# A trunk of two layers on one core: the norm factors spread by two products of rounded parts

## The chip, the core and the metric

The kernel runs on one core of a Trainium2 chip. A core has a matrix engine (TensorE, PE in the profile), three engines for elementwise work (VectorE as DVE, ScalarE as ACT, GpSimd as POOL) and queues that move data between the chip's memory and the core's on-chip memory. Each engine works through its own list of instructions in order and waits where an operand isn't ready. The metric is the time of one execution in microseconds (us), the median of several runs; lower is better.

## The reference, cut to what matters

The program is a decoder of two layers over 512 tokens of 1024 features. Each layer has a mixer (a convolution module in the first, differential attention in the second), a SwiGLU feed-forward, and a gate on a per-layer embedding. Feed-forward and gate begin with an RMS norm, and it is these norms that the change is about.

```
def rms_norm(x, g):
    xf = x.astype(jnp.float32)
    y = xf * lax.rsqrt(jnp.mean(xf * xf, axis=-1, keepdims=True) + EPS)
    return (y * g.astype(jnp.float32)).astype(x.dtype)
...
        u = rms_norm(h, ffn_norm_g[i])
        h = h + swiglu(u, ffn_w_gate[i], ffn_w_up[i], ffn_w_down[i])
        gate = jax.nn.sigmoid(rms_norm(h, ple_norm_g[i]) @ ple_w_gate[i])
        h = h + gate * (p[i] @ ple_w_proj[i])
```

The factor `rsqrt(mean(x*x) + EPS)` is one number for each token.

## The kernel before, in words

**Layout.** The hidden state lies transposed, as eight tiles `h[0]` to `h[7]` of 128 features by 512 tokens. A large product is made chunk by chunk of the output: `acc` in the matrix engine's result memory (a bank of tag `mm`, of which there are four) collects eight chunks of the input. Every fp32 operand is split into a rounded part `hi` and a rest `lo`, both of type `fp32r`, and `mm3` makes one chunk from three `fp32r` products: lines 166 (`lo` weights with `hi` input), 167 (`hi` with `hi`) and 168 (`hi` with `lo`). A weight tile is loaded to `wraw` (two buffers), rounded by ScalarE to `whi` (line 159, four buffers) and subtracted by VectorE to `wlo` (line 161, four buffers).

**The norm.** The products are made from the input times the gain, without the factor, and the factor is multiplied onto the result. `Norm.chunk` squares each chunk and GpSimd adds the squares up in `acc`. `columns` (line 199) multiplies four blocks of 128 tokens of `acc` with a matrix of ones, so that each token's sum stands in a partition; `rsqrt_cols` makes a 128x4 tile `r` of factors of it (VectorE, line 265; GpSimd's power, line 267). To have the factors along the free axis in all partitions, `diagonal` (line 272) multiplies the identity by the four columns of `r`, which gives a 128x512 tile of four diagonal blocks (a `wk` buffer), and `spread` (line 282) multiplies it with ones: each of the 128 rows of the result `tp` then holds all 512 factors. `rows` copies it to `rb` (ScalarE, line 257).

**Who uses it.** Five norms take this way: the first norm of all (the convolution's, through `diagonal` directly), and two in each layer by `Norm.diagonal` and `Norm.rows`: the feed-forward's, within the first pair of gate and up products of `ffn`, and the gate's, in `ple` behind its first two products. In `ffn`, `rb` is needed by lines 869 and 871, which take the results `pg` (gate) and `pu` (up) of a chunk out of their banks; in `ple` by line 912. While `rb` isn't there, the matrix engine goes on with the next chunks until the four banks are full. Lines 667 to 685 (`Operands.chunk`) prepare later operands from `rb` in the same stretch.

**Order.** A scheduler that estimates times when the program is built sets the order on each engine; on the chip each engine keeps that order. Tiles of one tag share a fixed number of buffers, and an instruction that writes a buffer waits for the readers of what it held before.

Of the kernel before, what the change touches and what calls it, by code (L numbers as in the profile page):

```python
# [12 lines left out]
F32 = mybir.dt.float32  # L13
F32R = mybir.dt.float32r
AF = mybir.ActivationFunctionType
ALU = mybir.AluOpType
# [4 lines left out]
P = 128  # L21
# [70 lines left out]
def trunk(ctx, tc, xT, pT, wts, diag, dww, vec, rel, onehot, lamv, out):  # L92
    nc = tc.nc
    V, A, G, T = nc.vector, nc.scalar, nc.gpsimd, nc.tensor
# [7 lines left out]
    def sb(shape, tag, bufs, dt=F32):  # L102
        uid[0] += 1
        return pool.tile(shape, dt, tag=tag, name=f"{tag}_{uid[0]}", bufs=bufs)
# [8 lines left out]
    wk = lambda dt=F32, shape=(P, S): sb(list(shape), "wk", 4, dt)  # L113
    big = lambda dt=F32, shape=(P, S): sb(list(shape), "big", 5, dt)
    f = lambda ap: ap.bitcast(F32)
# [12 lines left out]
    ones_r = sb([P, P], "ones", 1, F32R)  # L128
    ones = f(ones_r)
# [4 lines left out]
    t = wk()[:, 0:P]  # L134
# [4 lines left out]
    t = tp()  # L139
# [69 lines left out]
    class Norm:  # L209
# [39 lines left out]
            return rsqrt_cols(first_of(t), 4, 1.0 / D)  # L249

        def diagonal(self):
            self.dg = diagonal(self.columns())

        def rows(self):

            r = sb([P, S], "rb", 1)
            A.copy(r, spread(self.dg))
            return r
# [4 lines left out]
    def rsqrt_cols(src, n, inv):  # L263
        v = sb([P, P // 2], "v8", 2)[:, :8]
        last_v[0] = V.tensor_scalar(v[:, :n], src, inv, EPS, ALU.mult, ALU.add)
        r = sb([P, P // 2], "r8", 2)[:, :8]
        last_pow[0] = G.tensor_tensor(r[:, :n], v[:, :n], mhalf[:, :n], ALU.pow)
        return r[:, :n]

    def diagonal(r):  # L270
        dg = wk()
        V.tensor_tensor(
            dg.rearrange("p (b t) -> p b t", b=4),
            ident.unsqueeze(1).to_broadcast([P, 4, P]),
            r.unsqueeze(2).to_broadcast([P, 4, P]),
            ALU.mult,
        )
        return dg

    def spread(dg):  # L280
        t = tp()
        T.matmul(t, ones, dg, start=True, stop=True)  # L282
        return t


# [205 lines left out]
    for c in range(NC):  # L491
        wa, wg = pairs[c]
        if c == 0:
            pg = half(wg)
            pa = half(wa)
            norm.dg = diagonal(norm.columns_of_chunks(3))
            rb = norm.rows()
# [81 lines left out]
    r = rsqrt_cols(vs[:, 0:4], 4, 1.0)  # L579
# [4 lines left out]
    dg = wk()  # L584
# [360 lines left out]
    rl = sb([33, NH], "big", 5)  # L945
# [6 lines left out]
    for k in range(2):  # L952
        t = tp()
# [447 lines left out]
```

## Time and profile before

| what | value |
|---|---|
| median of 3 runs | 1247.7 us (1247.47 to 1248.56) |
| the profiled execution | 1246.62 us, of it 1244.5 us from the first instruction to the last (the span) |
| PE busy | 1234.6 us (99% of the span) |
| DVE busy | 877.2 us (70%) |
| ACT busy | 623.7 us (50%) |
| POOL busy | 469.7 us (38%) |
| spreads by line 282 | 5, recorded as 10 matmuls |
| diagonals by line 272 | 5, 0.69 us each |

A busy engine is one that works on an instruction; shares over the whole span hide that stages differ. A row of the timeline has the start, the duration, the engine, the line, the operation, what it writes and reads, and in brackets how long the engine had been idle and what ended the wait. A line number is that of the kernel before; the changed kernel's lines from 250 on stand five to nine lines lower (its spread by two products is line 291, its diagonal 277, its copy to `rb` 262, and 878 and 880 are what 869 and 871 were).

### The profile page before, as it was taken

To read this page: it belongs to the slowest core of one execution; us is meant where nothing else is said; L and a number is where in the kernel's file an instruction comes from. 1 tells how busy PE (TensorE), PEld (TensorE's weight loads), DVE (VectorE), ACT (ScalarE), POOL (GpSimd) and SP (SyncE) were. 2 spreads that over 40 slices of the span, in tenths; PEclk is the share of its full clock that TensorE was granted. 3 is DMA by queue.
4 is the path that set the end of the run, shared out by engine and by line. 5 is a ranking of instruction groups with operands and counts; after the bars stand their busy time and mean duration, and the time that the engine had idled before them with its cause. 6 is when DMAs were issued, how large, how long until landed. Compare 5 with 4: busy or idle time off the path is not lost.

```text
span 1244.5 us, 18421 instructions
## 1 busy us (share of the span) xinstructions
PE 1234.6 (99%) x7080; PEld 1081.8 (87%) x7080; DVE 877.2 (70%) x1230; ACT 623.7 (50%) x1096; POOL 469.7 (38%) x355
## 2 busy tenths in 40 slices
PE   9999999999999999999999999999999999999998
PEld 8888788888998899888888888788889998999887
DVE  6997865975895478547676876647966885588535
ACT  6652454533553255434566877735434552455432
POOL 3863432024670464132336635141026640562220
PEclk9999999999999999999999999999999999999999
DMA  7566224224323332334432330152232333232331
GB/s 267 185 213 195 77 57 121 90 100 125 96 92 119 102 94 77 102 104 152 124 114 80 104 100 29 52 153 85 90 127 90 102 114 109 83 102 87 104 98 67
DMA packets 49154, 136.33 MB, mean 110 GB/s; under 512 B 5635, under 2 KB 10243, under 8 KB 49068
## 3 DMA queue, kind: packets, MB, share of 16 engines
q1 hardware_dynamic: 46944, 131.74, 34.0%
q10 hardware_dynamic: 2124, 3.43, 0.9%
q8 instruction: 55, 0.90, 0.3%
q14 instruction: 31, 0.25, 0.1%
HBM read 128.84 MB, written 6.31 MB: 109 GB/s over the span
## 4 chain that ended last, share of the span: by engine, by line
PE 96%; DVE 2%; issue 1%; ACT 0%; POOL 0%; DVEq 0%; ACTq 0%; POOLq 0%
PE mm L166 29%; PE mm L167 29%; PE mm L168 29%; PE sc L398 2%; PE mm L1117 1%; PE tp L199 1%; PE sc L1085 1%; PE sc L1084 1%; PE tp L1104 1%; PE mm L398 1%; PE tp L1038 1%; PE mm L354 1%; DVE wlo L711 0%; PE tp L282 0%; PE tp L141 0%
## 5 line engine op out<-in xcount | busy, mean ns | idle before, releaser
L159 ACT CAST whi<-wraw 128x1024 fp32r<-128x1024 f32 (+2 forms) x145 | 145.6, 1013 | 218.3 <-PE mm L168 96.7
L161 DVE TENSOR_TENSOR wlo<-wraw,whi 128x1024 fp32r<-128x1024 f32 (+2 forms) x141 | 179.2, 1277 | 69.4 <-ACT whi L159 69.1
L166 PE MATMUL mm<-A,wlo 128*128 128x512 f32 (+1 forms) x568 | 222.1, 391 | 0.1
L167 PE MATMUL mm<-A,whi 128*128 128x512 f32 (+1 forms) x568 | 219.5, 387 | 0.0
L168 PE MATMUL mm<-A,whi 128*128 128x512 f32 (+1 forms) x568 | 217.3, 389 | 0.0
L166 PE MATMUL mm<-B,wlo 128*128 128x512 f32 x352 | 137.0, 389 | 0.0
L167 PE MATMUL mm<-B,whi 128*128 128x512 f32 x352 | 137.0, 389 | 0.0
L168 PE MATMUL mm<-B,whi 128*128 128x512 f32 x352 | 135.6, 389 | 0.0
L229 POOL TENSOR_TENSOR acc<-acc,wk 128x512 f32<-128x512 f32 x35 | 58.4, 1670 | 193.4 <-ACT wk L228 192.9
L166 PEld LDWEIGHTS mm<-A,wlo 128*128 128x128 f32 x568 | 106.8, 188 | 23.1 <-issue 1.4
L167 PE MATMUL mm<-C,whi 128*128 128x256 f32 x448 | 126.8, 283 | 0.0
L168 PE MATMUL mm<-C,whi 128*128 128x256 f32 x448 | 126.8, 283 | 0.0
L166 PE MATMUL mm<-C,wlo 128*128 128x256 f32 x448 | 126.8, 283 | 0.0
L167 PEld LDWEIGHTS mm<-A,whi 128*128 128x128 f32 x568 | 106.9, 188 | 22.0 <-issue 1.0
L168 PEld LDWEIGHTS mm<-A,whi 128*128 128x128 f32 x568 | 106.5, 188 | 22.0 <-issue 0.5
L711 DVE TENSOR_TENSOR wlo<-A,whi 128x1024 fp32r<-128x1024 f32 x60 | 105.7, 1769 | 19.1 <-ACT whi L710 19.1
L710 ACT CAST whi<-A 128x1024 fp32r<-128x1024 f32 x60 | 62.9, 1048 | 54.5 <-PE mm L168 43.3
L720 POOL TENSOR_TENSOR A<-wraw 128x512 f32<-128x512 f32 x16 | 22.5, 1408 | 170.4 <-DMA wraw<-in_wts 156.1
L720 POOL TENSOR_TENSOR A<-A 128x512 f32<-128x512 f32 x16 | 25.2, 1575 | 162.3 <-DMA A<-in_wts 162.3
L167 PEld LDWEIGHTS mm<-C,whi 128*128 128x128 f32 x448 | 86.0, 192 | 0.2
L166 PEld LDWEIGHTS mm<-C,wlo 128*128 128x128 f32 x448 | 86.0, 192 | 0.2
L168 PEld LDWEIGHTS mm<-C,whi 128*128 128x128 f32 x448 | 86.0, 192 | 0.0
(309 smaller groups left out, 3031.2 us busy)
## 6 DMA issues: line engine op xcount, KB each, us to landing
wraw<-in_wts SPq DMA_DIRECT2D x161, 512.0 KB, 3.6
A<-in_wts SPq DMA_DIRECT2D x32, 512.0 KB, 3.6
wraw<-in_wts SPq DMA_DIRECT2D x16, 384.0 KB, 3.1
D<-in_diag SPq DMA_DIRECT2D x22, 256.0 KB, 4.6
C<-in_diag SPq DMA_DIRECT2D x16, 256.0 KB, 5.1
h<-in_xT SPq DMA_DIRECT2D x8, 256.0 KB, 5.3
rest<-h SPq DMA_DIRECT2D x8, 256.0 KB, 2.4
bias<-scr ACTq DMA_DIRECT2D x8, 256.0 KB, 3.6
```

The lines of the kernel that those rows point to most:

```text
L159: A.copy(hi[:, cut], raw[:, cut])
L161: eng.tensor_tensor(lo[:, cut], raw[:, cut], f(hi[:, cut]), ALU.subtract)
L166: T.matmul(acc, al, bh, start=first, stop=False, **kw)
L167: T.matmul(acc, ah, bh, start=False, stop=False, **kw)
L168: return T.matmul(acc, ah, bl, start=False, stop=last, **kw)
L199: r = T.matmul(t[:, cut], src[:, cut], ones, start=first and b == 0, stop=last and b == 3)
L229: self.last = self.eng.tensor_tensor(self.acc, self.acc, sq, ALU.add)
L354: last_tap[0] = T.matmul(acc, dg[:, j % 4], ups[c][:, j : j + S], start=(j == 0), stop=(j == PE_TAPS[c] - 1))
L398: last_tap[0] = T.matmul(acc[:, g * P : (g + 1) * P], w, ups[c][:, g, LEAD - m : LEAD - m + P], start=(m == 0), stop=(m == LAGS - 1),)
L710: A.copy(hi, src)
L711: V.tensor_tensor(lo, src, f(hi), ALU.subtract)
L720: G.tensor_tensor(s[:, 0], r1[:, 0], r1[:, 1], ALU.add)
```

## The change

For the four norms of feed-forwards and gates, the 128x4 tile of factors is split into a rounded part `rh` and a rest `rl`; a diagonal is made of each, of type `fp32r`, and the spread is two `fp32r` products that add up in one bank. The first norm keeps the one fp32 product.

```
         def diagonal(self):
-            self.dg = diagonal(self.columns())
+            r = self.columns()
+            rh = sb([P, P // 2], "r8", 2, F32R)[:, :4]
+            rl = sb([P, P // 2], "v8", 2)[:, :4]
+            V.tensor_copy(rh, r)
+            V.tensor_tensor(rl, r, f(rh), ALU.subtract)
+            self.dg = diagonal(f(rh), F32R), diagonal(rl, F32R)
...
-    def diagonal(r):
-        dg = wk()
+    def diagonal(r, dt=F32):
+        dg = wk(dt)
         V.tensor_tensor(
             dg.rearrange("p (b t) -> p b t", b=4),
...
     def spread(dg):
         t = tp()
-        T.matmul(t, ones, dg, start=True, stop=True)
+        if not isinstance(dg, tuple):
+            T.matmul(t, ones, dg, start=True, stop=True)
+            return t
+        for i, d in enumerate(dg):
+            T.matmul(t, ones_r, d, start=i == 0, stop=i == 1)
         return t
```

The scheduler moves some instructions with it. On PE, at the first layer's feed-forward, `mm_1860` is the second chunk's gate product `pg`, `mm_1861` its `pu`, and `tp_1836` the spread. Before:

```order
L168 MATMUL mm_1860<-A_314_1714,whi_1849 128x512
L282 MATMUL tp_1836<-wk_1809,ones_70 128x512
L166 MATMUL mm_1860<-A_320_1752,wlo_1850 128x512
L167 MATMUL mm_1860<-A_320_1752,whi_1849 128x512
L168 MATMUL mm_1860<-A_320_1752,whi_1849 128x512
L166 MATMUL mm_1861<-A_286_1549,wlo_1856 128x512
```

Now, where the same two banks are called `mm_1867` and `mm_1868`:

```order
L168 MATMUL mm_1867<-A_314_1714,whi_1856 128x512
L166 MATMUL mm_1867<-A_320_1752,wlo_1857 128x512
L167 MATMUL mm_1867<-A_320_1752,whi_1856 128x512
L291 MATMUL tp_1842<-wk_1813,ones_70 128x512
L168 MATMUL mm_1867<-A_320_1752,whi_1856 128x512
L291 MATMUL tp_1842<-wk_1815,ones_70 128x512
L166 MATMUL mm_1868<-A_286_1549,wlo_1863 128x512
```

The spread's first product stands two products later than the one spread did, and its second behind the last product of the gate chunk.

On DVE, at the same place: `r` and `v` are the small 128x4 tiles, `wk` the diagonals, `wlo` the weights' rests, and lines 869 and 871 the first to use `rb`. Before:

```order
L265 TENSOR_SCALAR v_335_1805<-tp_1800 128x4
L161 TENSOR_TENSOR wlo_1939<-wraw_1937,whi_1938 128x1024
L272 TENSOR_TENSOR wk_1809<-ident_65,r_336_1807 128x512
L161 TENSOR_TENSOR wlo_1945<-wraw_1943,whi_1944 128x1024
L869 TENSOR_TENSOR big_1839<-mm_1774,rb_1835 128x512
L871 TENSOR_TENSOR big_1840<-mm_1775,rb_1835 128x512
L869 TENSOR_TENSOR big_1910<-mm_1860,rb_1835 128x512
L667 SCALAR_TENSOR_TENSOR B_354_1919<-h_7_87,vec_63,rb_1835 128x512
L667 SCALAR_TENSOR_TENSOR B_354_1919<-h_11_91,vec_63,rb_1835 128x512
L161 TENSOR_TENSOR wlo_2027<-wraw_2025,whi_2026 128x1024
```

Now:

```order
L270 TENSOR_SCALAR v_335_1805<-tp_1800 128x4
L161 TENSOR_TENSOR wlo_1946<-wraw_1944,whi_1945 128x1024
L255 CAST r_337_1809<-r_336_1807 128x4
L256 TENSOR_TENSOR v_338_1810<-r_336_1807,r_337_1809 128x4
L277 TENSOR_TENSOR wk_1813<-ident_65,r_337_1809 128x512
L277 TENSOR_TENSOR wk_1815<-ident_65,v_338_1810 128x512
L161 TENSOR_TENSOR wlo_1952<-wraw_1950,whi_1951 128x1024
L161 TENSOR_TENSOR wlo_2034<-wraw_2032,whi_2033 128x1024
L878 TENSOR_TENSOR big_1846<-mm_1774,rb_1841 128x512
L880 TENSOR_TENSOR big_1847<-mm_1775,rb_1841 128x512
L878 TENSOR_TENSOR big_1917<-mm_1867,rb_1841 128x512
```

Three instructions are new, and one subtraction of weights (`wlo_2027`, now `wlo_2034`) has moved from behind the first uses of `rb` to ahead of them.

On ACT, the copy to `rb` and the rounding of the same weight change places. Before:

```order
L159 CAST whi_1938<-wraw_1937 128x1024
L159 CAST whi_1944<-wraw_1943 128x1024
L257 COPY rb_1835<-tp_1836 128x512
L159 CAST whi_2026<-wraw_2025 128x1024
L870 ACTIVATE big_1839<-big_1839 128x512
```

Now:

```order
L159 CAST whi_1945<-wraw_1944 128x1024
L159 CAST whi_1951<-wraw_1950 128x1024
L159 CAST whi_2033<-wraw_2032 128x1024
L262 COPY rb_1841<-tp_1842 128x512
L879 ACTIVATE big_1846<-big_1846 128x512
```

The rounding now stands ahead of the copy. The other three norms change in the same way, the gates' with line 912 in the place of 869 and 871. In the lists of VectorE and ScalarE neighbours trade places over the 20 to 60 instructions behind each of these norms; all else keeps its order, GpSimd's list and the transfers' among it.

## The prediction

> **What bounds the kernel now.** I read the page first, its busy times, its slices and its chain.
>
> ```profile
> PE 1234.6 (99%) x7080; PEld 1081.8 (87%) x7080; DVE 877.2 (70%) x1230; ACT 623.7 (50%) x1096; POOL 469.7 (38%) x355
> ...
> PEclk9999999999999999999999999999999999999999
> ...
> PE 96%; DVE 2%; issue 1%; ACT 0%; POOL 0%; DVEq 0%; ACTq 0%; POOLq 0%
> ```
>
> The matrix engine works for 99% of the span at its full granted clock, and 96% of the chain that ended last is its own work. So a microsecond of matrix work that is taken out anywhere should come off the time, unless something else is late right behind it. The view of waits, for PE alone, tells how much else is late: seven groups, of which the first and two more are
>
> ```profile
> PE tp L141 <- POOL ident masks.py:199: 1.5, 1, 1.5
> PE sc L1084 <- DVE st L1087: 1.3, 2, 1.0
> ...
> PE mm L166 <- DVE big L768: 0.4, 1, 0.4
> ```
>
> None is at a norm's spread. The chain in order of time shows what the spreads cost on PE, beside two ordinary products:
>
> ```profile
> 27.84 0.86 PE tp L282 x2
> 171.76 0.45 PE mm L168 x2
> 217.35 0.86 PE tp L282 x2
> 565.89 0.86 PE tp L282 x2
> 862.01 0.86 PE tp L282 x2
> 1210.96 0.86 PE tp L282 x2
> ```
>
> All five spreads lie on the chain, with no wait in between. Each fp32 product of 128x512 appears as two records and takes 0.86 us of PE; two `fp32r` products of the same shape take 0.45 us.
>
> **The change part by part.** *The products.* Four of the five spreads (all but the one at 27.84) become two `fp32r` products each, with the same ones as weights. Such a product was never made with ones, but line 168's rows are of the same type, shape and number of columns, so I price it by them. A new pair costs 0.45 us and an old spread 0.86: 0.41 us saved each, 4 x 0.41 = 1.64 us. The bounds: if the second product came with the price of half an fp32 product, 0.43, the pair would cost 0.86 and nothing would be saved; if products between others gained as much as the neighbours of the old spread lose, the row of the product behind it helps:
>
> ```profile
> 216.97 0.39 PE L168 MATMUL mm<-A,whi 128*128 128x512 f32 x1
> 217.19 1.02 PE L282 MATMUL tp<-wk,ones 128*128 128x512 f32 x2
> 218.29 0.40 PE L167 MATMUL mm<-A,whi 128*128 128x512 f32 x1
> ```
>
> From the start at 216.97 to that at 218.29 are 1.32 us, in which two ordinary products (the L168 and an L166 that has a blurred record) and the spread were begun; two at 0.225 leave 0.87. So 0.42 us is the most: 1.68 us. I take 0.41.
>
> One page of the Trainium skill bears on this. "FP8 and Floating Point Precision", section "TensorE Precision Notes", has a true fp32 product make four passes through the array and the reduced one a single pass. By that rule the old spread would cost four of the trace's product steps, 4 x 0.227 = 0.91, and the saving would be 1.81 us instead of 1.64. The trace's 0.86 decides.
>
> *The chain to the diagonals.* VectorE gets three more instructions for each norm: a 128x4 rounding, a 128x4 subtraction and a second 128x512 diagonal. At the first feed-forward it looked so:
>
> ```profile
> 210.54 0.16 DVE L265 TENSOR_SCALAR v<-tp 128x4 f32<-128x4 f32 x1 [3.64 <-PE tp L199]
> 210.79 1.02 POOL L267 TENSOR_TENSOR r<-v,mhalf 128x4 f32<-128x4 f32 x1 [4.43 <-DVE v L265]
> 211.00 1.23 DVE L161 TENSOR_TENSOR wlo<-wraw,whi 128x1024 fp32r<-128x1024 f32 x1 [0.29 <-ACT whi L159]
> 212.14 0.69 DVE L272 TENSOR_TENSOR wk<-ident,r 128x512 f32<-128x512 f32 x1
> 214.21 1.22 DVE L161 TENSOR_TENSOR wlo<-wraw,whi 128x1024 fp32r<-128x1024 f32 x1 [1.39 <-ACT whi L159]
> 218.87 0.69 DVE L869 TENSOR_TENSOR big<-mm,rb 128x512 f32<-128x512 f32 x1 [3.43 <-ACT rb L257]
> 221.99 1.22 DVE L161 TENSOR_TENSOR wlo<-wraw,whi 128x1024 fp32r<-128x1024 f32 x1
> 224.06 0.42 DVE L680 TENSOR_TENSOR wtl<-B,wth 128x256 fp32r<-128x256 f32 x1
> ```
>
> The trace has no 128x4 rounding; the nearest row is L265's 0.16 us, and a 128x256 operation, 64 times as wide, took 0.42. So the two small ones cost 0.3 to 0.85 us and the second diagonal 0.69: 1.0 to 1.55 us, and I take 1.0. The second diagonal is then ready at 212.14 + 0.69 + 1.0 = 213.8 (at most 214.4). The scheduler begins the two products two and four products later than the old spread, at about 217.65 and 218.1. The margin is 3.7 us or more, so no product waits. On VectorE the 1.0 us and the weights' subtraction behind it (at 214.21 before) end by 216.5, in the 3.43 us of idle time that the row at 218.87 shows. That idle time is the cover; without it, the 1.0 us would push everything behind.
>
> *The factors come later.* This is the part that speaks against the change. On ScalarE the rounding of a weight now stands ahead of the copy to `rb`, and that rounding waited for PE:
>
> ```profile
> 218.25 0.59 ACT L257 COPY rb<-tp 128x512 f32<-128x512 f32 x1 [4.07 <-PE tp L282]
> 219.00 1.05 ACT L159 CAST whi<-wraw 128x1024 fp32r<-128x1024 f32 x1 [0.16 <-PE mm L168]
> ```
>
> It rewrites the weight buffer of the chunk in work, and so waits for that chunk's last product (L168), which now begins at 217.88 and ends about 0.39 later, so the rounding runs from 218.35 to 219.4. The copy ends at about 219.95 where it ended at 218.84: `rb` is 1.1 us late. On VectorE the subtraction that used to run at 221.99 is now ahead of L869 and ends at 220.55 (1.13 us to the next start). L869 then starts at 220.55 instead of 218.87, 1.7 us late, of which 1.13 is work only moved. Behind it wait the banks: the third chunk's gate product needs the bank that L869 empties, and began here:
>
> ```profile
> 224.22 0.39 PE L166 MATMUL mm<-A,wlo 128*128 128x512 f32 x1
> ```
>
> It would now begin at 224.22 - 0.41 = 223.8, and L869 ends at 221.2. The margin falls from 4.7 us to 2.6, and nothing waits. The weight's `lo` is made earlier than before, never later.
>
> *Where VectorE catches up.* It is 0.55 us behind, and PE 0.41 ahead, so it has to make good about 1 us. The busy times in the stretch behind the spread (columns: stretch, length, then PE, PEld, DVE, ACT, POOL busy, with counts) and a row of VectorE's timeline after it show where:
>
> ```profile
> 218.00:256.00 38.00, 38.00 (x169) 31.40 (x168) 36.06 (x59) 19.50 (x28) 0.00 (x0) 1.00 0.29 86
> 267.94 0.69 DVE L871 TENSOR_TENSOR big<-mm,rb 128x512 f32<-128x512 f32 x1 [3.57 <-PE mm L168]
> ```
>
> VectorE has 1.9 us free in the stretch, more than its lag, and by 267.94 it stands idle for 3.57 us, waiting for PE. From there on it starts when PE lets it, so the lag is gone and what follows moves ahead with PE.
>
> *The gates.* There the same exchange delays `rb` by as much, but the table load behind it was waiting anyway:
>
> ```profile
> 567.41 1.89 DVE L912 TENSOR_TENSOR big<-mm,rb 128x512 f32<-128x512 f32 x3 [3.88 <-ACT rb L257]
> 568.61 1.28 ACT L913 ACT_TABLE_LOAD   x1
> ...
> 1223.46 0.69 DVE L912 TENSOR_TENSOR big<-mm,rb 128x512 f32<-128x512 f32 x1 [1.06 <-PE mm L168]
> 1228.90 0.69 DVE L912 TENSOR_TENSOR big<-mm,rb 128x512 f32<-128x512 f32 x1 [2.63 <-PE mm L168]
> ```
>
> In the last gate VectorE waits for PE again from 1223.46 on, so the end of the program follows PE and keeps the saving.
>
> *The sum.* 4 x 0.41 = 1.64 us off, everything else hidden. The profiled execution took 1246.62 us (span 1244.5), so it would take 1244.98. The median of the three runs is 1247.7, 1.1 above that execution; against it, which is what will be measured, the forecast is 1247.7 - 1.64 = 1246.06, so 1246.1 us, 0.13% faster. About 0.2% (2.5 us) is what a measurement of this kernel can tell from no change, so this counts as the same.
>
> **The rivals.** *The saving is lost in the stretch where VectorE sets the pace.* At the end of the second part of the first feed-forward the chain leaves PE:
>
> ```profile
> 355.13 0.14 PE mm L168
> 355.35 1.06 ACT whi L710
> 373.73 0.34 DVE big L768
> 374.12 0.39 PE mm L166
> ```
>
> For 19 us the chain is VectorE's and ScalarE's, and PE waits 0.4 at its end. If VectorE's lag reached that far, what the first feed-forward saves would be lost there, and in the second layer likewise: 2 x 0.41 kept, 1246.9 us. Against it: the 3.57 us in which VectorE waits for PE in between, and that this chain begins with a PE product, so it moves ahead with PE.
>
> *The new products are no cheaper.* If `fp32r` products whose operand VectorE has just written in two halves, or which stand between others, cost 0.43 each, the time stays at 1247.7. The chain's 0.45 for two speaks against it.
>
> *Slower: the banks fill up.* If `rb` came so late that L869 emptied its bank after the third chunk wants it, PE would stand still at all four norms. The point from which this decides is a further 2.6 us of delay at a norm; to lose 2.5 us over all, the four waits have to add up to 2.5 + 1.64 = 4.1 us, so 3.6 us of further delay each. That gives 1247.7 - 1.64 + 4 x 1.1 = 1250.5. The new instructions cost 1.55 us at most and the waited-for PE product is known, so little speaks for it. GpSimd, from which VectorE could have to wait for a result, is not busy in the stretch from 218 to 256 (0.00).
>
> *More than 0.2% faster.* PE's waits behind VectorE could shrink with the new order. The 0.4 us above and as much in the second layer would bring 1247.7 - 1.64 - 0.8 = 1245.3; with the half microsecond by which medians of such runs differ (the three runs span 1.1) it crosses the bound.
>
> **How the numbers follow.** Forecast as worked out, 0.70 (1246.1, by itself 1245.2 to 1247.0); half the saving lost, 0.08 (1246.9); none saved, 0.04 (1247.7); slower by full banks, 0.06 (1250.5); faster with fewer waits, 0.12 (1244.8 to 1245.3). The range for 8 in 10 takes in the cases from 1244.7 to the 1248.3 that no saving and a slow median would give. Faster by over 0.2% (below 1245.2): the last case and a little of the forecast's spread, 0.14. Slower by over 0.2% (above 1250.2): 0.06. Within: 0.80.
>
> **What the profile after should show.** The four pairs on the chain with about 0.23 us a product, in the place of 0.86; L282's line left once, at 27.8. VectorE's diagonals ending 3 us or more ahead of the first product. `rb` about 1.1 us later behind its last product's place, L878 at the first feed-forward near 220.5, and PE with no wait there or at the third chunk. The third chunk's first product near 223.8, and everything behind earlier by 0.41, 0.82, 1.23 and 1.64 us. The prediction is wrong if PE waits for line 878 or 921 or for a diagonal, if a product of the pair takes 0.4, or if the shift shrinks between two norms.

## The result, and the profile after

The kernel after took 1246.28 us (median of 22 runs, 1244.99 to 1248.15); the kernel before, run beside it, 1248.41 us (median of 22, 1246.12 to 1252.41). The ratio is 0.998, with a 95% interval of 0.9973 to 0.9986: faster by 2.1 us between the medians and by 2.5 us by the ratio, whose interval is 1.7 to 3.4. The forecast was 1246.1 us and 1.64 us less than before.

The profiled execution of the kernel after seems to say otherwise. Its span is as long as that of before, 1244.7 us against 1244.5. These are the first rows of its page, the chain's shares, and two rows of PE's waits (PE's line, what it waited for, us in total, times, longest):

```profile
span 1244.7 us, 18430 instructions
...
PE 1232.4 (99%) x7080; PEld 1080.8 (87%) x7080; DVE 882.1 (71%) x1242; ACT 623.8 (50%) x1096; POOL 471.1 (38%) x355
...
PE 88%; DVE 4%; issue 2%; DMA 1%; ACT 0%; SPq 0%; POOL 0%; DVEq 0%; ACTq 0%
```

```profile
PE sc L407 <- DMA C<-pi: 1.7, 1, 1.7
...
PE mm L166 <- DVE big L777: 0.6, 2, 0.4
```

PE's busy time fell by 2.2 us, but it waited 1.7 us in the convolution for a transfer, which it did not do in the profile of before. The convolution ends with column sums on PE. The chain in order of time has them at these starts, in before and in after:

```profile
145.81 0.89 PE sc L199 x8
```

```profile
147.58 0.89 PE sc L199 x8
```

So after was 1.77 us late before it came to the first instruction that differs. From there to the end of the span are 1244.5 - 145.81 = 1098.7 us before and 1244.7 - 147.58 = 1097.1 after: 1.6 us less. The experiments are read by that stretch, since what lies ahead of it varies by itself.

The saving also arrives where the forecast had it, one step at each norm. The first feed-forward's column sums begin at 209.84 us before and at 211.65 after, 1.81 us late. With that taken off, the first gate's column sums begin 0.41 us earlier than before, those of the attention's norm, behind the first gate's spread, 0.86, the last gate's 1.21, and the end of the span comes 1.6 us earlier. Forecast were 0.41, 0.82, 1.23 and 1.64.

The new products are where the order put them, with the price of ordinary ones. The chain at the first feed-forward's norm, and at the first gate's:

```profile
219.39 0.23 PE mm L167
219.62 0.23 PE tp L291
219.85 0.23 PE mm L168
220.07 0.23 PE tp L291
220.30 0.23 PE mm L166
```

```profile
567.53 0.23 PE tp L291
568.21 0.23 PE tp L291
```

And what VectorE and ScalarE do at the first feed-forward, to be read against the rows of before after taking off the 1.8 us:

```profile
213.96 0.16 DVE L255 CAST r<-r 128x4 fp32r<-128x4 f32 x1
214.15 0.17 DVE L256 TENSOR_TENSOR v<-r,r 128x4 f32<-128x4 f32 x1
214.23 0.68 DVE L277 TENSOR_TENSOR wk<-ident,r 128x512 fp32r<-128x512 f32 x1
214.84 0.69 DVE L277 TENSOR_TENSOR wk<-ident,v 128x512 fp32r<-128x512 f32 x1
216.03 1.23 DVE L161 TENSOR_TENSOR wlo<-wraw,whi 128x1024 fp32r<-128x1024 f32 x1 [0.51 <-ACT whi L159]
221.24 1.23 DVE L161 TENSOR_TENSOR wlo<-wraw,whi 128x1024 fp32r<-128x1024 f32 x1 [3.99 <-ACT whi L159]
222.38 0.68 DVE L878 TENSOR_TENSOR big<-mm,rb 128x512 f32<-128x512 f32 x1
```

```profile
220.16 1.05 ACT L159 CAST whi<-wraw 128x1024 fp32r<-128x1024 f32 x1 [4.16 <-PE mm L168]
221.11 0.58 ACT L262 COPY rb<-tp 128x512 f32<-128x512 f32 x1
```

The second diagonal is ready at 215.53 and its product begins at 220.07. The copy to `rb` stands behind the weight's rounding, which waits for PE, and L878 behind that weight's subtraction. VectorE is idle for 3.99 us ahead of that subtraction all the same.

### The profile page after: what moved, and what is told of

Read it like the earlier page. It is cut to its first block, busy times and chain, and to the rows that moved or that the text cites. A ratio compares the mean times of both kernels' runs of the same rounds, so it can differ in the third digit from the quotient of the medians.

```text
span 1244.7 us, 18430 instructions
## 1 busy us (share of the span) xinstructions
PE 1232.4 (99%) x7080; PEld 1080.8 (87%) x7080; DVE 882.1 (71%) x1242; ACT 623.8 (50%) x1096; POOL 471.1 (38%) x355
## 4 chain that ended last, share of the span: by engine, by line
PE 88%; DVE 4%; issue 2%; DMA 1%; ACT 0%; SPq 0%; POOL 0%; DVEq 0%; ACTq 0%
PE mm L166 27%; PE mm L167 27%; PE mm L168 27%; PE mm L1126 1%; DVE sc L458 1%; PE sc L1094 1%; PE sc L1093 1%; PE tp L1113 1%; PE sc L407 1%; PE mm L407 1%; PE tp L1047 1%; PE mm L363 1%; PE tp L199 1%; DVE wlo L720 0%; DVE wlo L161 0%
```

## The experiments

All times are compared with runs of the kernel before on the same chip. The yardstick from the traces is the time from the convolution's column sums to the end of the span. In the kernel before it is 1098.7 us, in its repetition 1098.9; the differences are against 1098.8. Its own variation can be read from the table: where the four spreads are those of before it lies between 1098.4 and 1099.0, where they are those of after it is 1097.1 three times.

| kernel | ratio to before (95%) | column sums at | end of span | between | difference |
|---|---|---|---|---|---|
| before, again | 0.9996 (0.9987 to 1.0005) | 148.14 | 1247.0 | 1098.9 | +0.1 |
| after | 0.998 (0.9973 to 0.9986) | 147.58 | 1244.7 | 1097.1 | -1.7 |
| after, again | 0.9983 (0.9974 to 0.9991) | 148.01 | 1245.1 | 1097.1 | -1.7 |
| hi only | 0.9974 (0.9963 to 0.9984) | 147.24 | 1242.9 | 1095.7 | -3.1 |
| fp32 twice | 1.0028 (1.0016 to 1.0039) | 147.41 | 1249.4 | 1102.0 | +3.2 |
| VectorE's part only | 0.9998 (0.9989 to 1.0007) | 150.18 | 1249.2 | 1099.0 | +0.2 |
| power three times | 0.999 (0.9981 to 0.9999) | 147.60 | 1245.2 | 1097.6 | -1.2 |
| power five times | 1.0024 (1.0015 to 1.0033) | 148.68 | 1250.1 | 1101.4 | +2.6 |
| all five norms | 1.0001 (0.9992 to 1.001) | 149.75 | 1246.8 | 1097.1 | -1.7 |
| first norm only | 1.0022 (1.0013 to 1.003) | 150.46 | 1248.9 | 1098.4 | -0.4 |
| row sums, fp32 | 0.9976 (0.9965 to 0.9987) | 148.37 | 1243.0 | 1094.6 | -4.2 |
| row sums, two fp32r | 0.9951 (0.9938 to 0.9965) | 149.71 | 1243.2 | 1093.5 | -5.3 |

**The kernel before, unchanged.**

> The kernel before itself, unchanged, as a control. Products theory (the time moves by what the spreads' products cost on PE and by nothing else): ratio to before 1.000 within 0.07%. Rival, the convolution's transfers: in the profile of the kernel after, the first feed-forward's column sums began 1.81 us later than in the profile of before (211.65 against 209.84), though no instruction ahead of that place differs. If transfers within one execution do that, this kernel's profile too shows the column sums some tenths to 2 us away from 209.84, with the spreads still 0.86 us each.

The ratio is that of no change, and the profile's column sums begin 2.33 us later than in the first profile of the same code:

```profile
148.14 0.89 PE sc L199 x8
```

Its largest wait of PE is the one that the profile of after had, and before had not:

```profile
PE sc L398 <- DMA C<-pi: 2.0, 1, 2.0
```

Here `pi` is the detour of a convolution chunk through memory. So the convolution's length differs by 2.3 us between two executions of one program, with the transfer back from `pi` as the wait that shows. The first profile of before was a short one.

**The kernel after, unchanged.**

> The kernel after, unchanged, once more. Products theory: 1.64 us below before (ratio 0.9987, within 0.07%), and from the convolution's column sums to the end within 0.3 us of the first profile's 1097.1. Rival, something beside the products pays: the ratio stays at 0.998 or lower, as first measured.

1246.63 us, ratio 0.9983. The interval takes in 0.9987 and 0.998, so the timed runs don't tell the two expectations apart. The trace does as far as it goes: 1097.1 us from the column sums to the end, for the second time.

**One product instead of two.**

```
-            self.dg = diagonal(f(rh), F32R), diagonal(rl, F32R)
+            self.dg = (diagonal(f(rh), F32R),)
...
-            T.matmul(t, ones_r, d, start=i == 0, stop=i == 1)
+            T.matmul(t, ones_r, d, start=i == 0, stop=i == len(dg) - 1)
```

The rests `rl` are left out.

> The kernel after without the rests: one diagonal of the rounded factors and one product at the four norms, so the factors are those rounded to fp32r. Products theory: 4 x 0.227 = 0.91 us below the kernel after, 2.55 below before (ratio 0.9980); each of the four norms moves what is behind it by 0.63 us against before. Rival, the gain comes from the new order on VectorE and ScalarE and not from the products: no change against the kernel after (0.9983 to 0.9987).

**Both products in fp32.**

```
-            self.dg = diagonal(f(rh), F32R), diagonal(rl, F32R)
+            self.dg = diagonal(f(rh)), diagonal(rl)
...
-            T.matmul(t, ones_r, d, start=i == 0, stop=i == 1)
+            T.matmul(t, ones, d, start=i == 0, stop=i == 1)
```

> The kernel after with both products in fp32 (rounded parts and two diagonals as there). Products theory: two products of 0.86 us in the place of one, so 4 x 0.86 = 3.44 us above before (ratio 1.0028), each norm moving what is behind it by 0.86 us later. Rival, the gain comes from the new order: VectorE's new order is nearly that of the kernel after, so it would be at or below before (0.998 to 1.000).

These two are read best at the first gate, since between its column sums and those of the attention's norm lies only this one spread. The starts on the chain, for before, after, one product, and two fp32 products in turn (the last with its spreads):

```profile
557.51 0.89 PE tp L199 x8
609.22 0.89 PE tp L199 x8
```

```profile
558.91 0.89 PE tp L199 x8
610.17 0.89 PE tp L199 x8
```

```profile
558.34 0.89 PE tp L199 x8
609.37 0.89 PE tp L199 x8
```

```profile
559.83 0.89 PE tp L199 x8
568.44 0.86 PE tp L291 x2
569.53 0.86 PE tp L291 x2
612.40 0.89 PE tp L199 x8
```

The stretch is 51.71 us before, 51.26 after (0.45 less), 51.03 with one product (0.68 less) and 52.57 with two fp32 ones (0.86 more). A spread's price in time is the price of its products on PE, and the kernel with two fp32 products, whose new work on VectorE is the same as after's, is slower than before. The gain does not come from VectorE's new order. Over the whole stretch the two moved by 3.1 and 3.2 us where 2.55 and 3.44 were expected; the half microsecond too much with one product lies in the feed-forwards' stretches. There code that does the same work varies by as much: from the first feed-forward's column sums to the first gate's are 347.67 us in before, 347.98 in its repetition and 347.36 in the kernel with the first norm changed alone.

**VectorE's part alone.**

```
-            self.dg = diagonal(f(rh), F32R), diagonal(rl, F32R)
+            diagonal(f(rh))
+            self.dg = diagonal(r)
```

One fp32 product spreads the whole factors; the rounded part's diagonal and the rests are made and not used.

> The kernel before with the new work of VectorE alone: at the four norms the rounding, the subtraction and a second diagonal are made and not used, and the spread stays one fp32 product. Products theory: all of that is hidden behind PE, the time is that of before (ratio 1.000 within 0.07%), and no norm moves what is behind it. Rival, VectorE's cover is too short: up to 1.0 us more at each norm, 4 us in all (ratio up to 1.0032).

Ratio 0.9998, and the stretch at the first gate is 51.72 us against 51.71. VectorE's rows at the first feed-forward show the added work inside its idle time:

```profile
216.52 0.16 DVE L255 CAST r<-r 128x4 fp32r<-128x4 f32 x1
216.72 0.16 DVE L256 TENSOR_TENSOR v<-r,r 128x4 f32<-128x4 f32 x1
216.79 1.29 DVE L278 TENSOR_TENSOR wk<-ident,r 128x512 f32<-128x512 f32 x2
218.59 1.23 DVE L161 TENSOR_TENSOR wlo<-wraw,whi 128x1024 fp32r<-128x1024 f32 x1 [0.51 <-ACT whi L159]
```

It even waits 0.51 us behind it. The cover holds.

**Later factors.** GpSimd's power is made three times, and five times, over.

```
-        last_pow[0] = G.tensor_tensor(r[:, :n], v[:, :n], mhalf[:, :n], ALU.pow)
+        for _ in range(times):
+            last_pow[0] = G.tensor_tensor(r[:, :n], v[:, :n], mhalf[:, :n], ALU.pow)
...
-            r = self.columns()
+            r = self.columns(3)
```

The second kernel has `self.columns(5)`.

> The kernel after, with the power on GpSimd made three times over in the four norms instead of once (the same result), which makes the factors some 2 us later; the scheduler puts the two products 12 rows (2.7 us) later on PE for it. Products theory with the bank margin of 2.6 us as reckoned: the margin is just used up, PE waits 0 to 0.4 us before the third chunk, and the time is 0 to 1.6 us above the kernel after (ratio to before 0.9985 to 0.9998). Rival, the factors have no margin: about 2 us at each of the four norms, 8 us above the kernel after.

> The same with the power made five times over: some 4 us later, and the two products 17 rows (3.9 us) later on PE than in the kernel after. Products theory with the bank margin: L878 or L921 empties the first bank 1.2 to 1.5 us after PE wants it, so PE waits that long ahead of the third chunk of products behind the factors, at all four norms: 5 to 6 us above the kernel after (ratio to before 1.0025 to 1.0035). Rival, banks do not bind: the time stays that of the kernel after; rival, no margin at all: 16 us above it.

With three powers the yardstick rises by 0.5 us over after's, within what was expected, and by less than the feed-forwards' stretches vary; the timed ratio, 0.999, is inside too. With five it rises by 4.3 us, and the timed ratio, 1.0024, is just under what was expected.

The delays were larger than the 2 and 4 us expected. At the first feed-forward the power took 1.02 us in after, 3.39 made three times and 6.60 made five times, so the factors came 2.4 and 5.6 us later. What counts for the banks is the line that empties them: L878's counterpart (L879) began 1.5 and 2.65 us later than in after, counted from the feed-forward's column sums. The margin there is 2.5 us (it is read below), and the second of these just passes it: the chain goes through L879,

```profile
226.14 0.70 DVE big L879
```

and the third chunk's first product begins 0.43 us behind the product before it, where the step is 0.23. In the second feed-forward it is 0.44. At the gates L922 empties the banks. PE's waits show it (the kernel with five powers):

```profile
PE mm L166 <- DVE big L922: 1.0, 2, 0.5
...
PE mm L166 <- ACT whi L159: 0.6, 1, 0.6
...
PE tp L1048 <- POOL C L1061: 0.3, 1, 0.3
```

A wait in this view is shorter than what it costs, since a product's record is longer than the step from one product to the next. The first gate's wait of 0.50 us is a step of 0.89, and the last gate's is one of 0.88:

```profile
574.86 0.39 PE L168 MATMUL mm<-A,whi 128*128 128x512 f32 x1
575.75 0.50 PE L166 MATMUL mm<-A,wlo 128*128 128x512 f32 x1 [0.50 <-DVE big L922]
```

Beyond the usual step, the four are 1.7 us together. By stretches of PE's timeline, against after, the 4.3 us are 0.3 in the first feed-forward, 1.2 in the first gate, 1.4 in the attention, 0.7 in the second feed-forward and 0.8 in the last gate. Expected were 1.2 to 1.5 at each of the four norms and nothing in the attention. There 0.9 us of waits stands at the start, for a weight's rounding (line 159) and for GpSimd (line 1061). So the margin is real, PE begins to wait where it is used up, and lateness shows then in more places than the banks. What remains of the 4.3 us beyond these was not found in a wait.

**The first norm too.**

```
-            norm.dg = diagonal(norm.columns_of_chunks(3))
+            norm.dg = halves(norm.columns_of_chunks(3))
```

`halves` is the rounding, the subtraction and the two diagonals as the other norms have them.

> The kernel after, with the first norm's spread made of two products too. Products theory: another 0.41 us off, 2.05 us below before (ratio 0.9984), with the pair taking 0.45 us near 27 us and PE not waiting there. Rival, the convolution is paced by VectorE and transfers: the 0.41 us saved at 28 us is gone by the convolution's end (column sums of the convolution's norm at 145.8 us in before), so the time is that of the kernel after (ratio 0.9987). Rival, the chain to the diagonal is exposed at the start: PE waits up to 1 us at the first spread and the time is 0.6 us above the kernel after.

Ratio 1.0001: what the four norms gain is lost. From the column sums to the end the kernel is as fast as after, 1097.1 us, so the loss lies in the convolution. There the scheduler put six groups of transfers and VectorE's taps (the convolution's multiplications) in another order. On SP's queue after has this order at the first chunk that takes the detour through `pi`

```
L370 DMA pi_348<-big_346 128x512
L374 DMA C_75_350<-pi_348 32x4x128 x4
L155 DMA wraw_483<-in_wts 128x1024
L155 DMA wraw_489<-in_wts 128x1024
```

and the kernel with all five

```
L372 DMA pi_355<-big_353 128x512
L155 DMA wraw_490<-in_wts 128x1024
L376 DMA C_78_357<-pi_355 32x4x128 x4
L155 DMA wraw_496<-in_wts 128x1024
```

so that a weight's load now stands between the two halves of the detour. Whether the loss hangs on the first norm was tested next.

**The first norm only**, with the other four as before (`halves` in the first, one fp32 spread in the others).

> The kernel before with two products at the first norm alone. Its scheduled list of transfers in the convolution is that of the kernel with all five; the four other norms are as before. If all five were no faster because the first norm's change moves the convolution's transfers and VectorE's taps and costs 1.6 to 2 us there, this kernel is 1.6 to 2 us above before (ratio 1.0013 to 1.0016) and its convolution's column sums begin 1.5 us or more later than those of the unchanged kernels (145.8 to 148.1). Rival, that run of all five was chance: 0.41 us below before (0.9997).

1251.75 us, ratio 1.0022: 2.7 us slower than before by the ratio, 3.1 by the medians, with two products where one fp32 product was. Expected were 1.6 to 2. The column sums begin at

```profile
150.46 0.89 PE sc L199 x8
```

and PE waited longer for the same transfer:

```profile
PE sc L409 <- DMA C<-pi: 3.5, 1, 3.5
```

The wait is not the whole loss. Behind it PE runs the 72 matmuls of that chunk's convolution (line 398 in before, 409 here). In the repetition of before, in the kernel with all five and in this one they take, in turn:

```profile
108.12 8.28 PE sc L398 x72
```

```profile
108.32 9.90 PE sc L409 x72
```

```profile
109.31 9.62 PE sc L409 x72
```

From 110 to 115 us the granted clock was 1.00 in the first of these profiles, 0.75 in the second and 0.79 in the third. So of the 2.3 us by which this kernel's column sums begin later than those of before's repetition, 1.3 are the slower matmuls and 1.5 the longer wait, less the 0.41 saved. The same slower matmuls stand in the profile of VectorE's part alone (granted clock 0.77, 9.90 us): with a wait of 2.5 us they account for its column sums at 150.18, though its transfers have the order of before.

One such profile would prove nothing; the ratio over eleven runs does. Saving 0.4 us of PE at 28 us costs about 3 in the convolution. Which of the moved instructions does it was not tried, nor whether VectorE's three added instructions do a part of it by themselves.

**Another way to the factors.** Ones times the sums of squares give each token's sum in all partitions at once. This replaces the eight matmul records of the column sums, the diagonal and the spread; the root is then taken of 128x512 values.

```
         def diagonal(self):
...
+            t = tp()
+            T.matmul(t, ones, self.acc, start=True, stop=True)
+            self.dg = t
...
+                A.activation(r, self.dg, AF.Sqrt, scale=1.0 / D, bias=powers[:, 40:41])
+                V.reciprocal(r, r)
```

> Another way to the same factors at the four norms: one fp32 product of ones with the sums of squares gives each token's sum in all partitions at once, in the place of the eight records of column sums (0.89 us), the diagonals and the spread; ScalarE takes the square root and VectorE the reciprocal. Products theory: 0.89 + 0.45 - 0.86 = 0.48 us off at each norm against the kernel after, 1.92 in all, 3.6 below before (ratio 0.9971), if the root with its two table loads (1.28 us each) and the reciprocal are ready within the bank margin, which they have 5 us and more for. Rival: the table loads stand ahead of weights' roundings on ScalarE, or the reciprocal takes VectorE several us, and PE waits for weights or banks: as the kernel after or slower.

1245.18 us, ratio 0.9976 (0.9965 to 0.9987), and 4.2 us off the yardstick, where 3.6 were expected; no wait of PE stands at a norm. The constant for the bias, written at the program's start, also moved two groups of the convolution's transfers. The next kernel writes it behind the convolution and makes the product from two halves:

```
-            T.matmul(t, ones, self.acc, start=True, stop=True)
+            hi, lo = wk(F32R), wk(F32R)
+            A.copy(hi, self.acc)
+            V.tensor_tensor(lo, self.acc, f(hi), ALU.subtract)
+            T.matmul(t, ones_r, hi, start=True, stop=False)
+            T.matmul(t, ones_r, lo, start=False, stop=True)
```

> The row sums by products of ones with the sums of squares, these split into a rounded part and a rest (ScalarE and VectorE, 0.6 and 0.7 us, both idle there): two fp32r products in the place of one fp32 product, and the constant for the root's bias written behind the convolution, so that the convolution's transfers keep the order of before. Products theory: 0.89 + 0.86 - 0.45 = 1.30 us off at each of the four norms against before, 5.2 us in all (ratio 0.9958), 3.5 below the kernel after. Rival, the root, its table loads and the reciprocal of 3.35 us come 1.3 us later than in the run before and PE waits for banks: 0.9965 to 0.998.

1242.85 us against 1248.67, ratio 0.9951 (0.9938 to 0.9965): the fastest kernel here, about 6 us below before by the runs (five of this kernel) and 5.3 by the yardstick, where 5.2 were expected. VectorE's rows show the subtraction that makes the rest, the reciprocal and the first use of `rb` (L886), 71.5 us behind the convolution's column sums, where L878 in after stands 74.8 behind them:

```profile
210.94 0.69 DVE L255 TENSOR_TENSOR wk<-acc,wk 128x512 fp32r<-128x512 f32 x1
...
216.90 3.35 DVE L265 RECIPROCAL rb<-rb 128x512 f32<-128x512 f32 x1 [0.78 <-ACT rb L264]
...
221.25 0.68 DVE L886 TENSOR_TENSOR big<-mm,rb 128x512 f32<-128x512 f32 x1
```

## Why the prediction was right, point by point

*The products.* Priced at 0.45 us a pair against 0.86; they took 0.23 each, with the ones as weights and among other products. The stretch at the first gate became 0.45 us shorter, the last gate's to the end 0.40 (41.93 to 41.53). All four together give 1.7 us by the yardstick, twice, where 1.64 was forecast. That PE time is what counts, and not VectorE's new work or its order, is shown by the kernels with one product, with two fp32 ones and with VectorE's part alone.

*The chain to the diagonals.* The small operations took 0.16 and 0.17 us and the second diagonal 0.69, 0.9 us in all by their starts, where 1.0 was taken. The second diagonal was ready 4.5 us ahead of its product, where 3.7 or more was reckoned. Shown hidden by the kernel with VectorE's part alone.

*The later factors.* Less the 1.81 us by which its column sums begin later, `rb` was ready at 219.9 (reckoned 219.95) and L878 began at 220.57 (reckoned 220.55). The third chunk's first product began at

```profile
225.58 0.39 PE L166 MATMUL mm<-A,wlo 128*128 128x512 f32 x1
```

which is 223.8 less those 1.8 us, as reckoned, 2.5 us behind L878's end. No wait of PE appeared there. The margin is real and finite: L878's counterpart 1.5 us later cost 0.5 over the whole stretch and no wait there, 2.65 us later PE's step there grew by 0.2.

*Where VectorE catches up.* The forecast had VectorE's lag gone by the row that stood at 267.94 with 3.57 us of idle time. The same row after is

```profile
269.30 0.69 DVE L880 TENSOR_TENSOR big<-mm,rb 128x512 f32<-128x512 f32 x1 [3.57 <-PE mm L168]
```

Less 1.81 us this is 267.49, 0.45 earlier than before and as idle: VectorE follows PE again, as reckoned.

*The sum.* 1246.1 was forecast and 1246.28 measured. Part of that closeness is luck: the forecast started from a median of 1247.7 over three runs, and over 22 runs before took 1248.41. The difference, 2.1 us (1.7 to 3.4), is more than the 1.64 forecast, which lies just outside the first interval and inside the second series' (0.9974 to 0.9991). The yardstick finds 1.7. Whether the remaining half microsecond is real stays open; the convolution's variation, 2 us and more, is larger. The ratio also lies on the 0.2% that the prediction drew as the limit of what can be told from no change, while with 22 runs of each kernel the interval, 0.9973 to 0.9986, ends clear of 1: that limit was set too wide.

*What the prediction didn't see.* It took the stages ahead of the change for fixed, and named absolute starts (223.8 us for the third chunk) and shifts of 0.41 to 1.64 us. In the profile after, everything behind the convolution was 1.8 us late to begin with. Starts can only be compared within a stretch. It also took the chain's 96% PE in the first profile for the kernel's nature, while in the convolution PE's lead over VectorE and the transfers is so thin that the second profile of the same kernel, with 2.0 us of wait there, has PE at 86%.

*The rivals.* The stretch where VectorE sets the pace took nothing back that could be measured: from each feed-forward's column sums to the gate's behind it, after is 0.41 us shorter than before, in both layers. The prediction misread one row there. The 0.39 at 374.12 us is the product's own duration. The listed wait of 0.4 us for line 768 lies in the second layer, at 1019 us, and there is one of them; in the first layer PE stood still for less (a step of 0.43 us ends at 374.12, where 0.12 is usual), so 0.8 us was too much for the rival with fewer waits. After lists two such waits, 0.2 us in the first layer and 0.4 in the second, so that rival's gain did not come. The four passes of the Trainium skill ("FP8 and Floating Point Precision", section "TensorE Precision Notes"), by which 1.81 us was reckoned, can't be told from 1.64 by the timed runs. That section of the Trainium skill states the four passes; the single pass of the reduced kind is the prediction's reading of it. By the yardstick's 1.7 neither is wrong; the spreads that stayed fp32 took 0.86 us as the row had it, not the 0.91 that was estimated by that section.

## What to carry to other kernels

Where PE is the chain, price a product by a row of the same type and shape and count only PE's time, but name the engine that hides the rest and how many microseconds it has. Before reading two profiles against each other, find the first instruction that differs and compare from there: here the profiles' spans were equal while the kernel had become faster. And ask what the change does to a stage that PE does not lead: at the first norm the same change moved transfers and VectorE's work, and cost some seven times what it saved.

## What the runs showed of the hardware that was not expected

The convolution with its detour through memory took from 145.8 to 148.1 us in unchanged code ahead of its column sums, with one wait of PE for a transfer of 0 to 2.0 us. Behind that wait the granted clock was 0.75 to 0.79 from 110 to 115 us in four of the thirteen profiles, and the 72 matmuls there took 9.6 to 9.9 us; in the other nine it was 1.00 and they took 8.28. The four waits were 1.8, 2.5, 2.5 and 3.5 us, but waits of up to 2.3 us stand among the nine too, so the length of the wait alone does not decide it, and no run tells what does. VectorE's reciprocal of 128x512 values took 3.35 us, five times its multiplication of that size (0.68), and it was hidden all the same.
